# A decoder layer on one core: the gates' columns on ScalarE, a later place for the seventh mixed values, a new order in the first up tile, two more weight places

## The chip, the core and the metric

The kernel runs on one core of a Trainium2 chip. The metric is the device time of one execution in microseconds (us), the median of several runs. The engines are TensorE (PE in the profile: matmuls, and PEld: its weight loads), VectorE (DVE), ScalarE (ACT), GpSimd (POOL) and SyncE (SP), which issues nearly all of the DMAs.

## The reference

One decoder layer with 1024 rows of 1024 values, all in float32. Two groups of eight heads of 64 read one common input projection: sliding-window attention (window 128, two key heads, a sink per head) and forgetting attention, whose logits get the difference of running sums of log-sigmoid gates. Their outputs, joined to 1024 columns (the mixed values), go through `w_out` and are added to `x`. A feed-forward part with a squared ReLU follows.

```python
proj = jnp.einsum('bsd,de->bse', rmsnorm(x, attn_norm_g), w_in)
...
log_f = jax.nn.log_sigmoid(f_logit.astype(jnp.float32) + b_forget.astype(jnp.float32))
out_b = forgetting_attention(qb, kb, vb, log_f)
mixed = jnp.concatenate([out_a.reshape(b, s, A_Q_W), out_b.reshape(b, s, B_W)], axis=-1)
x = x + jnp.einsum('bse,ed->bsd', mixed, w_out)
hn = rmsnorm(x, mlp_norm_g)
hid = jnp.square(jax.nn.relu(jnp.einsum('bsd,df->bsf', hn, w_up)))
x = x + jnp.einsum('bsf,fd->bsd', hid, w_down)
```

## The kernel before

Every matrix product is made from two halves of each operand, a high one (the value rounded to the fp32r format) and a low one (the rest), in three matmuls: high by high, high by low, low by high. The function `split` makes the halves: a copy (ACT mostly) gives the high one, a subtraction (DVE or POOL) the low one. All matmuls of the products are recorded at line 73 and all splits of this function at lines 77 (ACT) and 80 (DVE, POOL), so that in the profile the tile names tell them apart.

The order of the instructions is not the order of the text. The program is traced, and a scheduler then lists each engine's instructions by priority and by the times that it expects; `high_priority` raises the priority of a block, and `issue_after(mark)` ties a block's instructions behind an earlier instruction of the same engine. On the chip every engine, and SP with its DMAs, follows its list in order.

**Input projection.** After the first 384 columns, `wa1_tile(t)` (line 458) projects row block t of 128 rows to 392 columns: 384 of queries and keys, and 8 that are the gates of the forgetting heads. `proj` uses two PSUM buffers in turn (pool `pd`), 24 matmuls each. ACT copies the 384 columns to `q3` (line 462). DVE reads the 8 columns, multiplies by the row's 1/rms (`rstd`), adds the bias `bfb`, and writes `z[:, :, t]` (line 463). The buffer is free when both have read it. `forget_gates` (line 470) turns `z` into running sums: a chain of DVE instructions on 64 columns, a transpose on PE (`ptf`, line 492), a scan, and a store to `c_d` (line 508).

**Attention** runs in units (scores, softmax, transposes, weighted sum), with the projections of the next heads, and later the first halves of the out projection, as fillers between them.

**Out projection.** For each of the eight column blocks dt, `out_first(dt)` does mixed blocks e = 0 to 3 beside the attention. `out_weights(dt, e0)` loads a piece of weights `wor` (two buffers), and splits it on ACT and POOL into a place w0 or w1, in turn. Places are slots of the pool `zw`, w0 to w6; a slot is given again when the last reader of its former tile is done. The variable i counts the pieces from 1; pieces 9 and 10 are those of dt = 0 and 4 with e = 4 to 7, whose products are spread by `beside(n, mark, e)` over the end of the attention, n being 0 or 1 for dt = 0 or 4. Six matmuls belong to each e. `drain` emits the waiting attention units, and `ended[-1]` is the last matmul of the newest of them. The seventh mixed values (e = 6) come through DRAM (`load_mix(6)`), the eighth (e = 7) straight from the last units. Pieces 11 to 16 follow for dt = 1, 5, 2, 6, 3, 7.

**The end of the out projection.** `out_finish(dt, ps)` adds the stored first half and writes h to DRAM. It then makes the inputs of the up projection, which uses Strassen's scheme (in Winograd's form) on 2 x 2 blocks: seven products whose right sides are sub-blocks of the scaled h (in `bh[1]`, `bh[2]`, `bh[3]`) and sums of them, t1 to t4, in `ts[:, 0]` to `ts[:, 3]`. Of each right side dt modulo 4 is a quarter. `ts[:, 0]` needs only dt below 4, the other sums need both halves. `sum_splits` splits a sum into `bh` and `bl`: sum 0 for product 5, 3 for 4, 1 for 6, 2 for 7. Before, all four are split when dt is 4 or more, and those for products 5 and 4 of the last quarter wait in `part["rest"]` until product 2 of the first up tile has been emitted. h of dt below 4 lies in w2, of dt 4 to 6 in w3.

**Up projection.** `up(j)` (16 tiles) makes four sums of weight blocks and then, in the order `UP = (1, 2, 3, 6, 7, 5, 4)`, splits the weights of each product into the next of the seven places (w5 first, then w6, w0, w1, w2, w3, w4), multiplies (12 matmuls, inputs in four quarters k) and adds the product into `u` and `b`.

**Down projection** follows, from about 784 us to the end.

Of the kernel before, what the change touches and what calls it, by code (L numbers as in the profile page):

```python
# [16 lines left out]
P = 128  # L17
# [38 lines left out]
def hybrid_layer(  # L56
# [89 lines left out]
    def slot(tag, name, shape, dt=F32, pool=None):  # L146
        pool = o[pool or ("zw" if tag[0] == "w" else "zl")]
        return pool.tile([P] + shape, dt, tag=tag, name=name, bufs=1)
# [309 lines left out]
    def wa1_tile(t):  # L458
        with paced():
            ps = proj(wa1, 392, t)  # L460
        with tc.high_priority(offset=HPA):
            nc.scalar.copy(q3[:, t, :], ps[:, :384])
            nc.vector.scalar_tensor_tensor(  # L463
                out=z[:, :, t], in0=ps[:, 384:392], scalar=rstd[:, t : t + 1], in1=bfb,
                op0=ALU.mult, op1=ALU.add,
            )
            if t % 2:
                qknorm(q3, 6, t - 1, t + 1)

    def forget_gates():  # L470
        zf = z.rearrange("p h t -> p (h t)")

        zt = ap2.tile([P, 4, NT * NH], F32, tag="sq", name="zt", bufs=1)
        ze, zs, zp = zt[:, 0], zt[:, 1], zt[:, 2]
        nc.vector.scalar_tensor_tensor(out=ze, in0=zf, scalar=-1.0, in1=zf, op0=ALU.mult, op1=ALU.min)
        nc.scalar.activation(ze, ze, AF.Exp)
        nc.vector.tensor_scalar(out=zs, in0=ze, scalar1=2.0, scalar2=None, op0=ALU.add)
        nc.vector.reciprocal(zs, zs)
        nc.vector.tensor_tensor(out=zs, in0=zs, in1=ze, op=ALU.mult)
        nc.vector.tensor_tensor(out=ze, in0=zs, in1=zs, op=ALU.mult)  # L480
        nc.vector.tensor_scalar_mul(zp, ze, 2.0 / 17.0)
        for n in (15, 13, 11, 9, 7, 5, 3):
            nc.vector.scalar_tensor_tensor(
                out=zp, in0=zp, scalar=2.0 / n, in1=ze, op0=ALU.add, op1=ALU.mult
            )
        nc.vector.scalar_tensor_tensor(out=zp, in0=zp, scalar=2.0, in1=zs, op0=ALU.add, op1=ALU.mult)
        nc.vector.scalar_tensor_tensor(
            out=zt[:, 3], in0=zf, scalar=0.0, in1=zp,
            op0=ALU.min, op1=ALU.subtract,
        )  # L490
        pt = pa.tile([P, 512], F32, tag="tr", name="ptf", bufs=3)
        nc.tensor.transpose(pt[: NH * NT, :P], zt[:, 3], ident)
        cum = ap2.tile([P, 256], F32, tag="mt", name="cum", bufs=2)[: NH * NT, :P]
        nc.vector.tensor_tensor_scan(
            out=cum, data0=ones1[: NH * NT].to_broadcast([NH * NT, P]),
            data1=pt[: NH * NT, :P], initial=0.0, op0=ALU.mult, op1=ALU.add,
        )
        off = pa.tile([P, 512], F32, tag="tr", name="off", bufs=3)
        mm(
            off[: NH * NT, 0:1], before.rearrange("p h t -> p (h t)"),  # L500
            cum[:, P - 1 : P], True, True,
        )
        offs = ap3.tile([NH * NT, 1], F32, name="offs")
        nc.vector.tensor_copy(offs, off[: NH * NT, 0:1])
        nc.vector.tensor_scalar(
            out=cum, in0=cum, scalar1=offs[:, 0:1], scalar2=None, op0=ALU.add
        )
        nc.sync.dma_start(c_d.rearrange("h (t q) -> (h t) q", q=P), cum)
# [357 lines left out]
    def out_weights(dt, e0):  # L866
        i = nout[0] = nout[0] + 1
        wr = o["zw"].tile([P, 4, P], F32, tag="wor", name="wor", bufs=2)
        nc.sync.dma_start(wr, w_o[dt][:, e0 : e0 + 4, :])
        w = slot(f"w{i % 2}", "wos", [2, 4, P], F32R)  # L870
        split(w[:, 0], w[:, 1], wr, nc.scalar, nc.gpsimd)
        return w[:, 0], w[:, 1]

# [51 lines left out]
    def beside(n, mark, *es):  # L925
        _, ps, w = ahead_of[n]
        with tc.issue_after(mark):
            out_products(ps, w, es)

    beside(0, marks[-1], 4, 5)  # L930
    beside(0, ended[-1], 6)
    beside(1, ended[-1], 4)
    drain(1)
    beside(1, ended[-1], 5)
    drain(0)
    beside(1, ended[-1], 6)
    for dt, ps, w in ahead_of:
        out_products(ps, w, [7])
# [25 lines left out]
    def out_finish(dt, ps):  # L964
        t, gain = dt % 4, gm[:, dt : dt + 1]
        h = slot(f"w{2 + dt // 4}", "h", [S]) if dt < 7 else rr
        with tc.issue_after(part["load"].ins) if dt == 7 else nullcontext():
            part["load"] = nc.sync.dma_start(h, part_d[dt])
        for c, cs in enumerate((left, right)):
            nc.vector.tensor_tensor(out=h[:, cs], in0=ps[c], in1=h[:, cs], op=ALU.add)  # L970
        nc.sync.dma_start(h_d[dt], h)
        if dt < 4:
            h_split(1, t, h[:, left], gain)
            ts = part["t"] = slot("m4", "ts", [4, 512])
            b12 = part["b12"] = slot("w4", "b12", [512])
            nc.scalar.activation(b12, h[:, right], AF.Copy, scale=gain)
            nc.vector.scalar_tensor_tensor(
                out=ts[:, 0], in0=h[:, left], scalar=gain, in1=b12, op0=ALU.mult, op1=ALU.subtract
            )
            return  # L980
        ts, b12 = part["t"], part["b12"]
        h_split(2, t, h[:, left], gain)
        h_split(3, t, h[:, right], gain)
        for i, q, other, op in (
            (1, right, ts[:, 0], ALU.add),
            (2, right, b12, ALU.subtract),
            (3, left, ts[:, 1], ALU.subtract),
        ):
            nc.vector.scalar_tensor_tensor(
                out=ts[:, i], in0=h[:, q], scalar=gain, in1=other, op0=ALU.mult, op1=op  # L990
            )
        part["rest"] = lambda: sum_splits(ts, t, ((0, 5), (3, 4)))
        sum_splits(ts, t, ((1, 6), (2, 7)))
        if t < 3:
            part.pop("rest")()
# [47 lines left out]
    def up(j):  # L1043
# [8 lines left out]
        minus(s[:, 3], a12, s[:, 1])  # L1052
        src = {1: a11, 2: a12, 3: s[:, 3], 4: a22, 5: s[:, 0], 6: s[:, 1], 7: s[:, 2]}
        m = {}
        for n in UP:
            w = w_slot("wu", [2, 4, P], F32R)
            split(w[:, 0], w[:, 1], src[n], nc.scalar, nc.vector if n in (2, 6, 5) else nc.gpsimd)
            m[n] = bank(f"pu{n}")
# [6 lines left out]
            if n == 1:  # L1065
                u = slot("m1", "u", [4, 512])
                b = slot("m2", "hb", [4, 512])
                nc.scalar.copy(u[:, 0], m[1])
            if n == 2:
                plus(b[:, 0], m[2], u[:, 0])  # L1070
            if n == 6:
                plus(u[:, 1], m[6], u[:, 0])
            if n == 7:
                plus(u[:, 2], m[7], u[:, 1])
            if n == 5:
                minus(u[:, 3], u[:, 1], m[5])
                minus(b[:, 2], u[:, 2], m[5])
                plus(b[:, 3], m[3], u[:, 3])
            if n == 4:
                plus(b[:, 1], m[4], u[:, 2])  # L1080
        return lambda: up_end(j, b)

    def up_end(j, b):
        nc.scalar.activation(b, b, AF.Relu)
# [273 lines left out]
```

## Time and profile before

| | |
|---|---|
| median of 3 runs | 1093.94 us (1093.51 to 1095.36) |
| profiled execution | 1094.93 us, its span 1093.2 us |
| granted clock of TensorE | 1.00 |
| DMA moved | 195.69 MB, 179 GB/s over the span |
| start of the first up product on PE | 476.59 us |
| start of the down products on PE | 783.96 us |

A row of the timeline has a start, a duration (both in us), the engine, the line, the operation, what it writes and reads, and a count where several were merged; in brackets stand the idle time before it and what ended it. A row of the waits has the total, the number of times and the longest.

### The profile page before, as it was taken

Reading aid. Unit: us, or ns where it says so; the run is one execution under the profiler, and the core shown is the slowest. Engines: PE = TensorE matmul, PEld = TensorE weight load, DVE = VectorE, ACT = ScalarE, POOL = GpSimd, SP = SyncE. Lnnn points to the kernel's source line nnn. Section 1 sums busy time; section 2 is a strip of 40 time slices with the busy share of each in tenths; the row PEclk is TensorE's granted clock in tenths of the full one; section 3 lists DMA queues with packets and bytes.
Section 4 is the critical chain, followed back from the end, with each engine's and each line's share of the span. In section 5 each row is a group of like instructions: output and inputs, shape, how many; then the busy total and the mean of one; then the engine's idle time right before and its main releaser. Section 6 shows DMA issues by size and latency. Waiting matters only on the chain.

```text
span 1093.2 us, 15691 instructions
## 1 busy us (share of the span) xinstructions
PE 1080.2 (99%) x5556; PEld 933.4 (85%) x5556; DVE 770.2 (70%) x1328; ACT 570.6 (52%) x1014; POOL 364.0 (33%) x352
## 2 busy tenths in 40 slices
PE   9999999999999999999999999999999999999998
PEld 8999999999998888888888888888888888888886
DVE  8377677766765676898686869665665877674395
ACT  5558588676765756554545453443633433333331
POOL 5572523435444544233223232332222222231100
PEclk9999999999999999999999999999999999999999
DMA  9401212324666465563554543344898876665423
GB/s 296 152 22 52 69 38 63 115 78 150 202 210 222 163 225 175 199 244 118 185 192 180 181 166 135 144 174 144 314 393 315 306 289 227 233 226 183 176 89 116
DMA packets 96223, 195.69 MB, mean 179 GB/s; under 512 B 7392, under 2 KB 19856, under 8 KB 96144
## 3 DMA queue, kind: packets, MB, share of 16 engines
q1 hardware_dynamic: 95856, 194.54, 51.4%
q8 instruction: 44, 0.72, 0.3%
q14 instruction: 35, 0.29, 0.1%
q10 hardware_dynamic: 288, 0.15, 0.0%
HBM read 141.61 MB, written 53.04 MB: 178 GB/s over the span
## 4 chain that ended last, share of the span: by engine, by line
PE 84%; DVE 6%; DMA 5%; issue 2%; ACT 2%; POOL 1%; SPq 0%; DVEq 0%; ACTq 0%
PE pu L73 28%; PE pd L73 27%; PE ps L73 12%; PE po L73 5%; PE spb L73 3%; PE pvb L73 3%; PE tpb L737 2%; PE sp L73 1%; PE pv L73 1%; DMA wr<-in_w_b_dram 1%; DMA xq<-in_x_dram 1%; PE tpa L566 1%; DVE x L217 1%; PE ptk L334 1%; DMA h_d<-h 1%
## 5 line engine op out<-in xcount | busy, mean ns | idle before, releaser
L73 PE MATMUL pd<-hx,wx 128*128 128x512 f32 (+1 forms) x1350 | 304.9, 388 | 0.0
L73 PEld LDWEIGHTS pd<-hx,wx 128*128 128x128 f32 x1350 | 252.7, 188 | 52.2
L73 PE MATMUL pu<-bh,wu 128*128 128x512 f32 x896 | 276.6, 390 | 0.5 <-ACT bh L959 0.5
L73 PE MATMUL ps<-w,x 128*128 128x384 f32 (+1 forms) x960 | 199.4, 345 | 1.5 <-DVE z L463 1.1
L73 PEld LDWEIGHTS pu<-bh,wu 128*128 128x128 f32 x896 | 168.1, 188 | 36.1 <-ACT bh L959 0.9
L73 PE MATMUL pu<-bl,wu 128*128 128x512 f32 x448 | 174.0, 389 | 0.0
L73 PEld LDWEIGHTS ps<-w,x 128*128 128x128 f32 x960 | 165.1, 189 | 5.0 <-DVE z L463 1.8
L77 ACT CAST hx<-hr 128x1024 fp32r<-128x1024 f32 x56 | 59.0, 1054 | 175.9 <-PE pd L73 169.9
L80 POOL TENSOR_TENSOR wx<-wda,wx 128x1024 fp32r<-128x1024 f32 x24 | 64.2, 2676 | 196.7 <-ACT wx L77 169.5
L80 DVE TENSOR_TENSOR hx<-hr,hx 128x1024 fp32r<-128x1024 f32 x56 | 72.6, 1305 | 72.6 <-ACT hx L77 72.6
L73 PEld LDWEIGHTS pu<-bl,wu 128*128 128x128 f32 x448 | 84.1, 188 | 17.6 <-issue 0.2
L73 PE MATMUL po<-mix,wos 128*128 128x512 f32 x384 | 95.0, 396 | 2.0 <-DMA mix<-mixs_d 1.1
L80 POOL TENSOR_TENSOR wu<-wus,wu 128x512 fp32r<-128x512 f32 x32 | 46.7, 1461 | 126.6 <-ACT wu L77 114.2
L73 PEld LDWEIGHTS po<-mix,wos 128*128 128x128 f32 x384 | 70.5, 188 | 16.7 <-ACT wos L77 1.5
L80 POOL TENSOR_TENSOR wu<-wur,wu 128x512 fp32r<-128x512 f32 x32 | 44.9, 1402 | 86.5 <-ACT wu L77 86.3
L77 ACT CAST wu<-wus 128x512 fp32r<-128x512 f32 x64 | 38.1, 617 | 62.3 <-PE pu L73 54.0
L1030 DVE TENSOR_TENSOR ht<-hb 128x512 f32<-128x512 f32 x32 | 21.8, 722 | 63.4 <-ACT hb L1085 63.4
L80 POOL TENSOR_TENSOR w<-wr,w 128x384 fp32r<-128x384 f32 (+1 forms) x47 | 51.3, 1100 | 41.3 <-ACT w L77 30.4
L406 DVE TENSOR_TENSOR ptl<-tpb,pth 128x512 fp32r<-128x512 f32 (+1 forms) x80 | 49.6, 631 | 21.9 <-ACT pth L405 18.7
L77 ACT CAST wx<-wda 128x1024 fp32r<-128x1024 f32 x56 | 58.5, 1049 | 7.1 <-DMA wda<-in_w_d_dram 7.1
L701 ACT ACTIVATE sb<-sb,nmb 128x128 f32<-128x128 f32 (+3 forms) x64 | 49.8, 778 | 22.5 <-DVE nmb L695 22.3
L405 ACT CAST pth<-tpb 128x512 fp32r<-128x512 f32 (+1 forms) x80 | 41.7, 543 | 16.9 <-PE tpb L737 11.0
(210 smaller groups left out, 1820.7 us busy)
## 6 DMA issues: line engine op xcount, KB each, us to landing
wda<-in_w_d_dram SPq DMA_DIRECT2D x34, 1024.0 KB, 8.8
hr<-hid_d SPq DMA_DIRECT2D x56, 512.0 KB, 5.9
wur<-in_w_u_dram SPq DMA_DIRECT2D x32, 512.0 KB, 4.3
hid_d<-ht SPq DMA_DIRECT2D x16, 1024.0 KB, 4.3
hid_d<-hb SPq DMA_DIRECT2D x16, 768.0 KB, 3.6
mix<-mixs_d SPq DMA_DIRECT2D x7, 1024.0 KB, 5.8
wr<-in_w_b_dram SPq DMA_DIRECT2D x32, 192.0 KB, 2.5
xq<-in_x_dram SPq DMA_DIRECT2D x8, 512.0 KB, 5.4
```

The costliest lines, as they stand in the source:

```text
L73: return nc.tensor.matmul(out, lhsT, rhs, start=start, stop=stop)
L77: hi_eng.copy(hi, src)
L80: lo_eng.tensor_tensor(out=lo, in0=src, in1=hi.bitcast(F32), op=ALU.subtract)
L217: last_x = nc.vector.scalar_tensor_tensor(out=lo, in0=xr[:, cs], scalar=ga, in1=hi.bitcast(F32), op0=ALU.mult, op1=ALU.subtract,)
L334: nc.tensor.transpose(pt[:w, j * P : (j + 1) * P], x[:, 4 * c + j, col : col + w], ident)
L405: nc.scalar.copy(hi[:, cols], pt[:, cols])
L406: nc.vector.tensor_tensor(out=lo[:, cols], in0=pt[:, cols], in1=hi[:, cols].bitcast(F32), op=ALU.subtract)
L566: nc.tensor.transpose(tp[:, hh * P : (hh + 1) * P], pts[hh // 2][:, hh % 2, c0 : c0 + P], ident)
L701: nc.scalar.activation(pr[:, :nk], pr[:, :nk], AF.Exp, scale=-1.0, bias=nm[:, c : c + 1], accum_out=dn_b[p % 2][:, h, i : i + 1] if p < 3 ...
L737: nc.tensor.transpose(tp[:, c0 : c0 + P], probs[qi][:, kb * P : (kb + 1) * P], ident)
L1030: eng.tensor_tensor(out=out, in0=a, in1=b, op=ALU.subtract)
```

## The change

Four edits. The 8 gate columns are read by ACT, scaled by `rstd`, and the bias is added later for all 64 columns at once by DVE. The six products of dt = 0 with e = 6 move behind the last drained unit. Pieces 11 and 12 of the out weights get the places w6 and w5. In the first up tile product 5 comes second; the sums of products keep their former order, each as soon as all before it are there (`todo`, `up_sums`), and sum 0 of each quarter (t1) is split when dt is below 4.

```diff
         with tc.high_priority(offset=HPA):
             nc.scalar.copy(q3[:, t, :], ps[:, :384])
-            nc.vector.scalar_tensor_tensor(
-                out=z[:, :, t], in0=ps[:, 384:392], scalar=rstd[:, t : t + 1], in1=bfb,
-                op0=ALU.mult, op1=ALU.add,
+            nc.scalar.activation(
+                z[:, :, t], ps[:, 384:392], AF.Copy, scale=rstd[:, t : t + 1]
             )
...
     def forget_gates():
+        nc.vector.tensor_tensor(
+            out=z, in0=z, in1=bfb.unsqueeze(2).to_broadcast([P, NH, NT]), op=ALU.add
+        )
...
-        w = slot(f"w{i % 2}", "wos", [2, 4, P], F32R)
+
+        w = slot(f"w{i % 2 + (5 if i in (11, 12) else 0)}", "wos", [2, 4, P], F32R)
...
     beside(0, marks[-1], 4, 5)
-    beside(0, ended[-1], 6)
     beside(1, ended[-1], 4)
     drain(1)
     beside(1, ended[-1], 5)
     drain(0)
+    beside(0, ended[-1], 6)
     beside(1, ended[-1], 6)
...
                 out=ts[:, 0], in0=h[:, left], scalar=gain, in1=b12, op0=ALU.mult, op1=ALU.subtract
             )
+            sum_splits(ts, t, ((0, 5),))
             return
...
-        part["rest"] = lambda: sum_splits(ts, t, ((0, 5), (3, 4)))
+        part["rest"] = lambda: sum_splits(ts, t, ((3, 4),))
...
-        for n in UP:
+        todo = list(UP)
+        for n in UP if j else (1, 5, 2, 3, 6, 7, 4):
             w = w_slot("wu", [2, 4, P], F32R)
...
             if n == 1:
                 u = slot("m1", "u", [4, 512])
                 b = slot("m2", "hb", [4, 512])
-                nc.scalar.copy(u[:, 0], m[1])
-            if n == 2:
-                plus(b[:, 0], m[2], u[:, 0])
...
+            while todo and todo[0] in m:
+                up_sums(todo.pop(0), m, u, b)
         return lambda: up_end(j, b)
+
+    def up_sums(n, m, u, b):
+        if n == 1:
+            nc.scalar.copy(u[:, 0], m[1])
+        if n == 2:
+            plus(b[:, 0], m[2], u[:, 0])
...
```

The rest of `up_sums` is the former list of sums, unchanged.

More of the change, by code (lines that the diff above doesn't have):

```diff
@@ L1067, in up @@
                 b = slot("m2", "hb", [4, 512])
-                nc.scalar.copy(u[:, 0], m[1])
-            if n == 2:
-                plus(b[:, 0], m[2], u[:, 0])
[L1071 to L1080, printed above, removed]
-        return lambda: up_end(j, b)
+            while todo and todo[0] in m:
+                up_sums(todo.pop(0), m, u, b)
+        return lambda: up_end(j, b)
+    def up_sums(n, m, u, b):
[3 more added lines that the diff above has]
+            plus(b[:, 0], m[2], u[:, 0])
+        if n == 6:
+            plus(u[:, 1], m[6], u[:, 0])
+        if n == 7:
+            plus(u[:, 2], m[7], u[:, 1])
+        if n == 5:
+            minus(u[:, 3], u[:, 1], m[5])
+            minus(b[:, 2], u[:, 2], m[5])
+            plus(b[:, 3], m[3], u[:, 3])
+        if n == 4:
+            plus(b[:, 1], m[4], u[:, 2])
     def up_end(j, b):
```

## The prediction

> **What bounds the kernel now.** The page comes first: the busy times of the engines.
>
> ```profile
> span 1093.2 us, 15691 instructions
> PE 1080.2 (99%) x5556; PEld 933.4 (85%) x5556; DVE 770.2 (70%) x1328; ACT 570.6 (52%) x1014; POOL 364.0 (33%) x352
> ```
>
> PE is the bound, and the change leaves its matmuls as many and as long as they were. So the change can win only where PE stands idle, 13.0 us in all. Next come PE's own waits.
>
> ```profile
> PE ps L73 <- DVE z L463: 1.1, 2, 0.8
> PE po L73 <- DMA mix<-mixs_d: 1.1, 1, 1.1
> PE po L73 <- ACT wos L77: 1.0, 2, 0.7
> PE pu L73 <- ACT bh L959: 0.5, 1, 0.5
> PE sp L73 <- DVE z L463: 0.5, 1, 0.5
> ```
>
> The columns are total, times and longest. Each of the four edits has its counterpart here: z is the gates' column, mix the mixed values, wos the weight places, bh the inputs of the first up tile. Then the windows say whether time won would last.
>
> ```profile
> 428.00:445.00 17.00, 15.22 (x84) 12.56 (x85) 9.91 (x19) 8.49 (x18) 2.26 (x7) 1.00 0.27 99
> ...
> 470.00:480.00 10.00, 9.49 (x43) 7.53 (x41) 10.00 (x17) 5.65 (x10) 0.00 (x0) 1.00 0.82 273
> ...
> 784.00:1084.00 300.00, 300.00 (x1325) 248.40 (x1324) 198.64 (x175) 113.12 (x113) 59.40 (x22) 1.00 0.67 240
> ```
>
> Columns: PE, PEld, DVE, ACT, POOL, clock, DMA share, GB/s. The clock is full. The last 300 us before the end are PE alone without a gap: what PE wins earlier ends at the end of the kernel. In 470 to 480 DVE is busy without a gap as well, so there an edit that gives DVE more to do early can cost.
>
> **Edit 1: the gates' columns go to ScalarE.** The timeline of PE shows the three waits, those of ACT and DVE what lies at the second and third.
>
> ```profile
> 47.77 2.94 PE L73 MATMUL ps<-w,x 128*128 128x392 f32 x15 [0.34 <-DVE z L463]
> ...
> 68.76 3.29 PE L73 MATMUL ps<-w,x 128*128 128x392 f32 x17 [0.80 <-DVE z L463]
> ...
> 78.95 0.36 PE L73 MATMUL sp<-k1a,q1a 128*128 128x256 f32 x1 [0.47 <-DVE z L463]
> ```
>
> ```profile
> 66.88 0.21 ACT L297 ACTIVATE sr<-ss 128x12 f32<-128x12 f32 x1
> 67.12 0.48 ACT L462 COPY q<-ps 128x384 f32<-128x384 f32 x1
> ```
>
> ```profile
> 68.48 0.23 DVE L463 SCALAR_TENSOR_TENSOR z<-ps,rstd,vt 128x8 f32<-128x8 f32 x1
> ...
> 78.72 0.09 DVE L545 DVE_READ_ACCUMULATOR2_ANT nm_a<- 128x1 f32 x1
> 78.72 0.23 DVE L463 SCALAR_TENSOR_TENSOR z<-ps,rstd,vt 128x8 f32<-128x8 f32 x1
> ```
>
> The projection has two PSUM buffers, and each is free only when both readers are done: the copy of 384 columns (ACT) and z (DVE). For the fifth row block ACT is through by 67.60, but z stands in DVE's queue until 68.48 and ends at 68.71; PE, out of work at 67.96, starts at 68.76. With z behind the copy on the same engine, the buffer is free by 67.12 + 0.48 + 0.21 = 67.81, before PE asks. The price of z on ACT is not in the trace; the nearest row, an ACT instruction of 12 columns, takes 0.21 against 0.23 on DVE. The bounds are 0.21 and the 0.48 of the whole copy; I take 0.21. Even at 0.48 the buffer is free at 68.08, and 0.12 of the wait stays. So 0.34 + 0.80 go. The third wait names z, yet the scores need a buffer that L545 frees; its last piece ends at 78.81 and PE starts at 78.95. Between nothing and 0.47, I take the difference of those two, 0.14. Sum of this edit: 1.28.
>
> The Trainium skill, "ScalarE: Activation LUTs", section "Rules for kernel authors", speaks against it: additions and multiplications belong on VectorE, which is up to about three times faster per element in bf16. By that rule alone z on ACT would cost three times its 0.23, and at 67.60 + 0.69 = 68.29 the second wait would keep 0.33. The rows do not agree (0.21 beside 0.23), because so short an instruction is not paid by the element; the rule would leave the edit at 0.95 instead of 1.28.
>
> The bias is now added to all 64 columns by one more DVE instruction at the head of the gates. Its price is that of the last instruction of the same shape:
>
> ```profile
> 120.13 0.23 DVE L487 SCALAR_TENSOR_TENSOR zt<-z,zt 128x64 f32<-128x64 f32 x1
> ...
> 122.42 0.27 PE L492 MATMUL ptf<-ident,zt 128*64 128x128 f32 x1
> ```
>
> The work that hides it is PE's projection: PE turns the gates 2.06 us after DVE has them. Without that cover it would cost 0.23.
>
> **Edit 2: the seventh mixed values last.** Timeline of PE, then of DVE, then the chain that ended last.
>
> ```profile
> 433.30 1.55 PE L73 MATMUL po<-mix,wos 128*128 128x512 f32 x6
> 435.91 1.66 PE L73 MATMUL po<-mix,wos 128*128 128x512 f32 x6 [1.06 <-DMA mix<-mixs_d]
> 437.40 0.28 PE L73 MATMUL pvb<-pth,vb 128*128 128x256 f32 x1
> ...
> 438.84 4.27 PE L73 MATMUL po<-mix,wos 128*128 128x512 f32 x18
> ```
>
> ```profile
> 433.95 0.56 DVE L406 TENSOR_TENSOR ptl<-tpb,pth 128x384 fp32r<-128x384 f32 x1 [0.77 <-ACT pth L405]
> ```
>
> ```profile
> 430.90 4.97 DMA mix<-mixs_d
> ```
>
> At 434.85 PE runs dry, since the next six products need the seventh mixed values, whose load lands at 435.87. Behind them stand twelve products of the last attention unit (437.40 to 438.84 by their starts, 1.44 us), whose operands are complete at 433.95 + 0.56 = 434.51. The change puts these twelve in front: they fill 434.85 to about 436.3, the load has landed, and the whole 1.06 goes. The margin is 436.3 - 435.87 = 0.4 us; a load later than that is waited for again. The mixed values of the last unit must now be ready after twelve more products (six before), so they have more cover than they had.
>
> **Edit 3: two more weight places.**
>
> ```profile
> 443.80 32.95 PE L73 MATMUL po<-mix,wos 128*128 128x512 f32 x144 [0.69 <-ACT wos L77]
> ```
>
> ```profile
> 443.15 1.12 ACT L77 CAST wos<-wor 128x512 fp32r<-128x512 f32 x2
> ```
>
> ```profile
> 422.18 0.33 SPq L869 DMA_DIRECT2D wor<-in_w_o_dram  x1
> ```
>
> ```profile
> DMA to landing us min/median/max: 2.9/3.7/7.9
> ```
>
> The last line is from the view of the tile wor. Weight pieces 11 and 12 were loaded by about 426 (422.18 + 3.7), but their places w1 and w0 held pieces 9 and 10 until PE's last product. In w6 and w5 nothing lies, and the two casts can run any time before 443. The 0.69 goes. POOL's half of the splitting moves with them:
>
> ```profile
> 443.83 3.08 POOL L80 TENSOR_TENSOR wos<-wor,wos 128x512 fp32r<-128x512 f32 x2 [10.07 <-ACT wos L77]
> ```
>
> ```profile
> 445.68 1.78 DVE L977 SCALAR_TENSOR_TENSOR ts<-h,vt,b 128x512 f32<-128x512 f32 x1
> ...
> 454.77 0.75 DVE L977 SCALAR_TENSOR_TENSOR ts<-h,vt,b 128x512 f32<-128x512 f32 x1
> ```
>
> The same DVE instruction takes 1.78 beside POOL and 0.75 without it, so the move gives a full DVE about 1.0 us back. I book none of it, as PE does not wait there. The Trainium skill, "GPSIMD Engine Reference", Specifications, has GpSimd share its SBUF interfaces with VectorE, in conflict with instructions of two SBUF inputs; the two rows agree. By that rule the earlier place does little harm, as the evictions of the attention tail (L406) read PSUM and only one SBUF input.
>
> **Edit 4: the first up tile in the order 1, 5, 2, 3, 6, 7, 4, with product 5's inputs split as soon as t1 is there.**
>
> ```profile
> 476.59 0.39 PE L73 MATMUL pu<-bh,wu 128*128 128x512 f32 x1
> ...
> 479.98 0.73 PE L73 MATMUL pu<-bh,wu 128*128 128x512 f32 x2 [0.51 <-ACT bh L959]
> ```
>
> ```profile
> 478.68 0.62 ACT L77 CAST wu<-wus 128x512 fp32r<-128x512 f32 x1 [1.80 <-DMA h_d<-h]
> 479.21 0.72 ACT L959 ACTIVATE bh<-h,vt 128x512 fp32r<-128x512 f32 x1
> ...
> 486.06 0.63 ACT L77 CAST wu<-wus 128x512 fp32r<-128x512 f32 x1 [1.25 <-DMA h_d<-h]
> ```
>
> PE waits for the fourth quarter of bh1, and that stands on ACT behind the cast of product 5's weights, which waits until h has left place w3. Now product 5 has w6, free long before, and nine of its products need only the first three quarters: 9 x 0.229 (32.95 / 144) = 2.06 us of cover for a wait of 0.51. It goes. Against it: PE comes 1.06 + 0.69 = 1.75 us earlier than before, while DVE, full, has its start moved by the 1.06 alone; the 0.69 are inside the 2.06 as well. DVE gets four low halves earlier, but three of them leave its list before the last h, so one (about 0.7 us) stands ahead; again covered.
>
> What is late next is place w2: product 7 used it, now product 6 does, one product earlier. It was free at 486.06. By the order of the text PE asks for it at 476.59 - 1.75 + 48 x 0.229 = 485.8, so the wait is 486.06 + 0.63 - 485.8 = 0.9 if h leaves no earlier, and nothing if it moves along with PE. Near the lower end, for h's sums come at least 1.06 earlier: I take 0.3.
>
> **Sum.** 1.28 + 1.06 + 0.69 + 0.51 = 3.54, less 0.3: 3.2 us. The profiled execution took 1094.93 us, 1.7 more than its span; it becomes 1091.7. It lies 1.0 above the median of the runs (1093.94), so the median becomes 1090.7.
>
> **Rivals.** About 0.2%, or 2.2 us, is what a measurement of this kernel can tell from no change.
>
> *New waits in the old places.* Product 6 pays its full 0.9 at w2, and the weight loads that now go earlier share the DMA engines with the load of the seventh mixed values. Two pieces of 256 KB (128 x 4 x 128 values of 4 bytes) at the 273 GB/s of the window of 470 to 480 take 1.9 us; if the load loses all of that, PE waits 1.9 - 0.4 = 1.5. The gain shrinks to 3.54 - 2.4 = 1.1: 1092.8. For it: ACT's 1.80 and 1.25 on h. Against it: in 428 to 445 the DMA engines are busy 0.27 of the time.
>
> *The time won at the gates is lost again.*
>
> ```profile
> 137.25 0.44 PE L73 MATMUL ps<-w,x 128*128 128x384 f32 x1 [0.31 <-ACT w L77]
> ```
>
> Here PE waits for weights whose load stands on SP behind the store of the gates' sums. If that chain kept its hour, this wait would grow by 1.28 and the gain would be 1.9: 1092.0. Against it: the chain goes through PE's own list (ptf at 122.42) and moves along.
>
> *Slower.* SP issues in order. The loads of pieces 13 and 14 wait until POOL has split 11 and 12, and these may now stand on SP ahead of the load of the seventh mixed values. That decides if the split of piece 11 stays late on ACT: at 441 the load would land at 441 + 5.0 = 446 instead of 435.87, PE would stand about 9.7 us from 436.3, and the kernel would take 6.2 us longer: 1100. From 5.8 us of delay on (3.54 + 2.2) it is slower by over 0.2%. Against it: these casts are free to run by 426, and ACT has room.
>
> *The change doesn't do what it says.* The order is worked out by a scheduler with times of its own; the trace shows the first tile's products already interleaved. If the two reorderings change nothing on PE (1.06 and 0.51 stay), the gain is 1.7: 1092.3. Against it: the six products are tied behind the last unit's mark, so they cannot stay.
>
> **How the numbers follow.** The forecast 0.64; new waits 0.11; lost at 137 0.09; no reordering 0.08; slower 0.08. Faster by over 0.2% is the forecast, within 0.2% are the three in the middle: 0.28. The range: down to 1089.2 (all of 3.87 with the third z wait whole, the 0.4 by which the fastest run lies under the median, and 0.5 for waits that the reshuffled schedule may drop), up to 1093.3 (new waits, with 0.5 for waits that it may add). It leaves out the slower case and some 0.1 at the ends.
>
> **What would show it.** Right: no PE wait on z, none on mix after 434, none on wos near 443, none on bh L959; the out products begin about 1.75 us earlier against the attention's end. Wrong: PE waits on DMA mix again, on ACT wu in the first up tile, or a larger wait on ACT w near 137; for the slower case a load of mix issued on SP behind two of wor.

## The result and the profile after

The change made the kernel slower. The median is 1099.86 us (1098.77 to 1100.64, 8 runs) against 1094.45 us of the kernel before in the same comparison (1093.42 to 1098.77, 8 runs): a ratio of 1.0045, interval 1.0034 to 1.0056. The forecast was 3.2 us faster; it came out 5.4 us slower. The profiled execution took 1100.15 us.

Two lines of the page of the kernel after, the span and the engines' busy times:

```profile
span 1098.4 us, 15693 instructions
...
PE 1083.5 (99%) x5556; PEld 938.1 (85%) x5556; DVE 776.2 (71%) x1321; ACT 573.7 (52%) x1022; POOL 369.6 (34%) x352
```

The span grew by 5.2 us. PE idles 14.9 us instead of 13.0 (the span less its busy time), and is busy 3.3 us longer with as many matmuls: more than half of the loss lies in matmuls that became slower. The waits of PE after (total, times, longest):

```profile
PE pu L73 <- ACT bh L962: 3.3, 1, 3.3
PE tpb L739 <- DVE ptl L406: 2.6, 3, 1.8
PE qps L73 <- DVE warm L191: 1.3, 1, 1.3
PE spb L73 <- DVE nmb L697: 0.8, 1, 0.8
PE pvb L73 <- DVE mtb L756: 0.7, 2, 0.5
```

Every wait that the four edits aimed at in the earlier part is gone: none on z, none on mix, none on wos. In their place stand two new ones: on `ptl`, the low half of the transposed probabilities near the end of the attention, and on `bh`, where 0.5 became 3.3. The windows around both (PE, PEld, DVE, ACT, POOL, clock, DMA share, GB/s):

```profile
415.00:430.00 15.00, 12.27 (x70) 10.19 (x69) 11.81 (x26) 10.42 (x23) 8.88 (x13) 0.89 0.46 158
480.00:490.00 10.00, 6.69 (x23) 5.19 (x22) 8.30 (x14) 5.71 (x10) 1.87 (x2) 0.83 0.72 281
```

PE loses 2.7 of 15 and 3.3 of 10 us, and the granted clock falls to 0.89 and 0.83. The timeline of PE shows what that does:

```profile
78.56 0.35 PE L73 MATMUL sp<-k1a,q1a 128*128 128x256 f32 x1 [0.46 <-DVE nm_a L547]
...
417.34 0.66 PE L739 MATMUL tpb<-ident,sb 128*128 128x128 f32 x4 [1.80 <-DVE ptl L406]
...
419.23 0.58 PE L73 MATMUL pvb<-pth,vb 128*128 128x256 f32 x1 [0.55 <-DVE mtb L756]
419.61 0.41 PE L73 MATMUL pvb<-ptl,vb 128*128 128x256 f32 x1
...
477.37 0.39 PE L73 MATMUL pu<-bh,wu 128*128 128x512 f32 x1
...
483.57 1.05 PE L73 MATMUL pu<-bh,wu 128*128 128x512 f32 x2 [3.31 <-ACT bh L962]
484.41 0.63 PE L73 MATMUL pu<-bl,wu 128*128 128x512 f32 x1
...
487.54 0.39 PE L73 MATMUL pu<-bl,wu 128*128 128x512 f32 x1
```

After the 3.31 us a matmul takes 0.63 and not 0.39, and one starts every 0.43 us instead of every 0.23; from 487.54 they are fast again. Eight matmuls at 0.2 us too much are 1.6 us on top of the wait. The same is seen from 419.61: 0.41 where such a matmul takes 0.28. What held the two producers up stands in ACT's timeline:

```profile
413.10 0.62 ACT L77 CAST wos<-wor 128x512 fp32r<-128x512 f32 x1 [3.77 <-DMA wor<-in_w_o_dram]
...
415.98 0.59 ACT L405 CAST pth<-tpb 128x512 fp32r<-128x512 f32 x1
...
417.71 0.62 ACT L77 CAST wos<-wor 128x512 fp32r<-128x512 f32 x1 [1.15 <-DMA wor<-in_w_o_dram]
...
482.27 0.62 ACT L77 CAST wu<-wus 128x512 fp32r<-128x512 f32 x1 [2.77 <-DMA h_d<-h]
482.80 0.72 ACT L962 ACTIVATE bh<-h,vt 128x512 fp32r<-128x512 f32 x1
```

In both places ACT stands still in front of a cast whose input, or whose place, is not there yet, and the eviction or the input that PE needs stands behind that cast. At 413.10 it is the cast of piece 11, for 3.77 us: edit 3 let it go ahead of piece 10's, and its load, the eleventh of `wor`, was issued only at 408.95. At 417.71 it is that of piece 12; at 482.27 it is the cast of product 7's weights into w3, which waits until h of column block 6 has left that place. SP's timeline has the load and, further on, that write of h:

```profile
408.95 0.38 SPq L871 DMA_DIRECT2D wor<-in_w_o_dram  x1
...
474.96 0.32 SPq L974 DMA_DIRECT2D h_d<-h  x1
475.37 2.89 SPq L1016 DMA_DIRECT2D wur<-in_w_u_dram  x4
```

The write was issued at 472.21 before and at 474.96 now, 2.4 us instead of 4.4 ahead of the first up product, with four weight loads right behind it in both kernels. The cast came 6.5 us behind it before (478.68) and 7.3 now.

### The profile page after: what moved, and what is told of

Read it like the earlier page. It is cut to its first block, busy times and chain, and to the rows that moved or that the text cites. A ratio compares the mean times of both kernels' runs of the same rounds, so it can differ in the third digit from the quotient of the medians.

```text
span 1098.4 us, 15693 instructions
## 1 busy us (share of the span) xinstructions
PE 1083.5 (99%) x5556; PEld 938.1 (85%) x5556; DVE 776.2 (71%) x1321; ACT 573.7 (52%) x1022; POOL 369.6 (34%) x352
## 4 chain that ended last, share of the span: by engine, by line
PE 89%; DMA 5%; DVE 3%; issue 1%; ACT 1%; SPq 1%; POOL 0%; DVEq 0%; ACTq 0%; POOLq 0%
PE pu L73 28%; PE pd L73 27%; PE ps L73 14%; PE po L73 4%; PE qps L73 3%; PE pvb L73 3%; PE spb L73 3%; PE tpb L739 2%; PE sp L73 1%; PE pv L73 1%; PE tpa L568 1%; DMA h_d<-h 1%; PE ptk L334 1%; DMA wur<-in_w_u_dram 1%; DMA wor<-in_w_o_dram 1%
## 5 line engine op out<-in xcount | busy, mean ns | idle before, releaser
L80 POOL TENSOR_TENSOR wu<-wur,wu 128x512 fp32r<-128x512 f32 x32 | 49.7, 1555 | 105.0 <-ACT wu L77 105.0
L697 DVE CUSTOM_DVE_ANT_0 sb<-spb,cb 128x512 f32<-128x512 f32 (+2 forms) x64 | 37.2, 584 | 22.5 <-PE spb L73 17.4
```

Of the source, the lines that this page charges most:

```text
L80: lo_eng.tensor_tensor(out=lo, in0=src, in1=hi.bitcast(F32), op=ALU.subtract)
L697: nc.vector.tensor_tensor_reduce(out=pr[:, c * 512 : c * 512 + n], in0=sp[:, :n], in1=cb[:, c * 512 : c * 512 + n], scale=1.0, scalar=3e38 ...
```

## The experiments

Each was compared with the kernel before on its own chip, in five rounds; three chips were used, so the ratios compare better than the microseconds. Three repairs are made with `issue_after`: it only sets the order in one engine's list, behind a named instruction. T: ScalarE's casts of pieces 11 and 12 behind its copy in the last attention unit. W: the cast of product 7's weights (w3) in the first up tile behind `bh2` of the last column block. S: the weight sums of the first up tile on VectorE behind the adds of h of block 2. The fourth, L, moves the low half of product 4's weights in the first tile from POOL to VectorE.

| kernel | contents | median us | ratio to before, interval |
|---|---|---|---|
| gates_only | edit 1 | 1092.30 | 0.9972, 0.9961 to 0.9983 |
| mixed_last_only | edit 2 | 1094.10 | 0.9993, 0.9979 to 1.0007 |
| places_only | edit 3 | 1099.01 | 1.0032, 1.0018 to 1.0045 |
| up_order_only | edit 4 | 1098.24 | 1.0022, 1.0010 to 1.0033 |
| gates_and_mixed | edits 1, 2 | 1093.38 | 0.9983, 0.9973 to 0.9993 |
| places_tied | edit 3, T | 1097.30 | 1.0024, 1.0014 to 1.0035 |
| places_sums_later | edit 3, T, S and product 2's split | 1096.23 | 1.0012, 0.9999 to 1.0025 |
| up_order_low4_vector | edit 4, L | 1094.03 | 0.9997, 0.9982 to 1.0012 |
| gates_w3_later | edit 1, product 5's cast moved | 1093.74 | 0.9986, 0.9977 to 0.9996 |
| after_tail_casts_tied | all, T | 1094.65 | 1.0005, 0.9995 to 1.0015 |
| w3_later | all, W | 1096.65 | 1.0020, 1.0011 to 1.0029 |
| all_repaired | all, T, W, L | 1093.07 | 0.9982, 0.9972 to 0.9991 |
| all_repaired_sums | all, T, W, L, S | 1091.65 | 0.9965, 0.9953 to 0.9977 |
| all_repaired_sums_2 | the same, another chip | 1091.70 | 0.9974, 0.9963 to 0.9984 |
| mended_without_order | edits 1, 2, 3, T, S and product 2's split | 1093.39 | 0.9991, 0.9982 to 1.0001 |
| mended_without_places | edits 1, 2, 4, W, L | 1091.99 | 0.9973, 0.9962 to 0.9983 |

### One edit at a time

**gates_only**

```diff
-            nc.vector.scalar_tensor_tensor(out=z[:, :, t], ...
+            nc.scalar.activation(z[:, :, t], ps[:, 384:392], AF.Copy, scale=rstd[:, t : t + 1])
```

> Edit 1 alone: the gates' columns are read by ScalarE, nothing else is changed. Theory A (the loss comes from casts that stand in ScalarE's list ahead of other work and wait for a transfer: the weight casts of pieces 10 to 12 in the attention tail, and the cast of product 7's weights ahead of bh1): edit 1 has no part in it, the waits on z go, 1.2 us faster than before, PE waits between 405 and 440 no larger than before. Rival B (any edit near the front reshuffles the attention stage, and that is what costs): 1.5 to 2.5 us slower, with new PE waits in the attention tail.

Measured: 0.9972, more gained than either theory had. The gain was had although a wait grew; the waits of PE:

```profile
PE pu L73 <- ACT bh L961: 2.1, 1, 2.1
...
PE po L73 <- ACT wos L77: 0.7, 1, 0.7
```

No wait on z and none on mix is left. Edit 1 does what the prediction said, and it reshuffles the attention. The mix wait need not have gone by that: it is missing in up_order_only too, whose lists are those of the kernel before until past 460 us. The old 0.5 on bh has become 2.1, probably as PE comes earlier.

**mixed_last_only**

```diff
-    beside(0, ended[-1], 6)
     beside(1, ended[-1], 4)
...
+    beside(0, ended[-1], 6)
     beside(1, ended[-1], 6)
```

> Edit 2 alone: the six products with the seventh mixed values behind the last attention unit. Both theories: the wait of 1.06 us on the load of mix goes, 1.0 us faster; theory B would allow a loss only if other waits in the tail change.

Measured: 0.9993, which cannot be told from no change, nor from the forecast 1.06 us (0.1%). PE has the order that was meant, and the wait on mix is gone from the profile. But this wait comes and goes by itself: with the lists of the kernel before it is 1.06 there, 0.84 in places_tied and missing in up_order_only, so the profile doesn't show that the edit removed it.

**places_only**

```diff
-        w = slot(f"w{i % 2}", "wos", [2, 4, P], F32R)
+        w = slot(f"w{i % 2 + (5 if i in (11, 12) else 0)}", "wos", [2, 4, P], F32R)
```

> Edit 3 alone: places w6 and w5 for weight pieces 11 and 12. Theory A: the casts of pieces 11 and 12 move on ScalarE into the attention tail ahead of evictions and wait there for their load; PE waits on DVE ptl of 1.5 us or more between 410 and 425, followed by a time of slow matmuls; 1.5 to 3 us slower in spite of the 0.7 won at wos. Rival B: 0.7 us faster.

Measured: 1.0032. ACT's timeline has the casts ahead of the softmax and the evictions, waiting for their loads:

```profile
419.19 0.62 ACT L77 CAST wos<-wor 128x512 fp32r<-128x512 f32 x1 [1.33 <-DMA wor<-in_w_o_dram]
...
424.75 0.62 ACT L77 CAST wos<-wor 128x512 fp32r<-128x512 f32 x1 [2.10 <-DMA wor<-in_w_o_dram]
```

PE pays for it in four waits of 0.5 to 0.9 us at 428 to 433, on `dnb` and `ptl`, later than expected; and it has two waits of 1.0 us in the first up tile, which no theory had. The profiled execution, 1101.12 us, is the slowest of the seven.

**up_order_only**

```diff
-        for n in UP:
+        for n in UP if j else (1, 5, 2, 3, 6, 7, 4):
```

(with the sums and splits of the change's last hunks)

> Edit 4 alone: first up tile in the order 1, 5, 2, 3, 6, 7, 4. Theory A: the cast of product 7's weights stands ahead of bh1 on ScalarE and waits until h has been written; the PE wait on bh1 is as long as before (0.5) or longer, up to 3 us if the write of h is late, with slow matmuls behind it; between 0 and 3 us slower. Rival B: the cover of nine products of number 5 removes the wait, 0.5 us faster.

Measured: 1.0022. The wait on bh did not go, and a larger one came, neither theory's. The timelines of PE and of POOL:

```profile
479.04 0.73 PE L73 MATMUL pu<-bh,wu 128*128 128x512 f32 x2 [0.77 <-ACT bh L959]
...
495.71 0.73 PE L73 MATMUL pu<-bh,wu 128*128 128x512 f32 x2 [2.31 <-POOL wu L80]
```

```profile
486.65 9.00 POOL L80 TENSOR_TENSOR wu<-wur,wu 128x512 fp32r<-128x512 f32 x2 [6.76 <-ACT wu L77]
```

PE waits for the low weights of product 4. They are the second of these two subtractions on POOL, which take 9.00 us together and 1.3 each when VectorE leaves POOL alone. The first belongs to another product, and most of the time is its own: in up_order_low4_vector below, where product 4's has left POOL, it still takes 6.99. So here too an instruction that PE doesn't need yet stands in front.

### Taking the suspects away

**places_tied**

```diff
-        split(w[:, 0], w[:, 1], wr, nc.scalar, nc.gpsimd)
+        with tc.issue_after(copies[-1]) if i in (11, 12) else nullcontext():
+            split(w[:, 0], w[:, 1], wr, nc.scalar, nc.gpsimd)
```

> Edit 3 alone, as in places_only, but ScalarE's casts of pieces 11 and 12 are tied behind ScalarE's copy in the last attention unit (the places w6 and w5 and all else stay). Theory A (in places_only the casts stand in ScalarE's list ahead of the attention's evictions and wait there for their loads, and this makes TensorE wait): the waits of 0.5 to 0.9 us on ptl and dnb at 428 to 433 go, no wait on wos near 443 either, and the loss of 0.32% is gone: a ratio of 0.999 to 1.000, 1094 to 1095.5 us. Theory B (the places themselves, the earlier work of POOL or the loads of pieces 13 and 14 cost): it stays near 1.003, with the same waits; or a new wait on wor 13 and 14, whose loads now start about 20 us later, near 445 to 450.

Measured: 1.0024, a miss. The lists up to the end of the attention are those of the kernel before, and no wait on `ptl` or `dnb` over 0.6 is left; but the waits in the first up tile stay, and with them most of the loss. VectorE's timeline ahead of it:

```profile
466.06 1.31 DVE L80 TENSOR_TENSOR wu<-wur,wu 128x512 fp32r<-128x512 f32 x1 [0.73 <-ACT wu L77]
467.30 1.77 DVE L1035 TENSOR_TENSOR wus<-wur 128x512 f32<-128x512 f32 x1
469.00 0.68 DVE L1032 TENSOR_TENSOR wus<-wur 128x512 f32<-128x512 f32 x1
469.60 1.28 DVE L972 TENSOR_TENSOR h<-po,h 128x512 f32<-128x512 f32 x2
```

Three instructions of the first up tile now stand ahead of both adds of h of block 2; before, one of them stood between the adds and two behind. The first waits 0.73 for its cast, two are stretched to about 1.3 and 1.8 beside POOL. (This profile too is of the slowest of the seven executions, 1100.20 us.) All that VectorE has to do for h comes later, while PE comes earlier.

**places_sums_later**

```diff
+        with tc.issue_after(part["h2"]) if j == 0 else nullcontext():
             plus(s[:, 0], a21, a22)
...
+            with tc.issue_after(part["h2"]) if j == 0 and n == 2 else nullcontext():
                 split(w[:, 0], w[:, 1], src[n], ...
```

> Edit 3 with the tied casts of places_tied, and in addition the four weight sums of the first up tile and the split of its product 2 tied, on VectorE, behind the adds of h of column block 2 (on ScalarE nothing changes). In places_tied these come ahead of the adds: VectorE waits 0.7 us for the cast of product 2's weights, two of the three instructions are stretched to 1.3 and 1.8 us beside POOL, h of blocks 2 and 6 comes 1.2 to 1.5 us later, and TensorE waits 1.2 on bh and 1.1 on bl in the first up tile. Theory D (these three instructions in VectorE's list are edit 3's loss): the wait on bh goes to 0.5 or less, bl under 0.5, and the ratio falls from 1.0024 to 0.999 to 1.0005. Theory B (the later places of POOL's and ScalarE's work cost by themselves): the waits stay over 1 us each and the ratio at 1.002 or more.

Measured: 1.0012 (0.9999 to 1.0025), half way. PE's timeline in the first up tile:

```profile
481.89 0.73 PE L73 MATMUL pu<-bh,wu 128*128 128x512 f32 x2 [0.43 <-ACT bh L961]
...
492.38 0.73 PE L73 MATMUL pu<-bh,wu 128*128 128x512 f32 x2 [1.13 <-POOL wu L80]
```

The waits on bh and bl fell as theory D had it, but POOL is next: a wait of 1.13. So these three instructions are a part of the loss, and behind them there is another late engine.

**up_order_low4_vector**

```diff
-            ... nc.vector if n in (2, 6, 5) else nc.gpsimd)
+            ... nc.vector if n in (2, 6, 5) or n == 4 and j == 0 else nc.gpsimd)
```

> Edit 4 alone as in up_order_only, but the low half of product 4's weights in the first up tile is made by VectorE (0.68 us) and not by POOL; the lists are otherwise the same there. Theory P (edit 4's loss is POOL's subtraction, stretched from 1.3 to about 4.5 us beside a full VectorE): the wait of 2.3 us on POOL wu goes and with it the stretch of half clock behind it (14 matmuls of 0.43 instead of 0.23, some 2.5 us): ratio from 1.0022 to 0.9985 to 1.0. Theory Q (another instruction is as late: VectorE's own list): a wait of 1 us or more at the same product, ratio over 1.001.

Measured: 0.9997, theory P. The wait of 2.3 is gone, and with it the slow stretch (nine matmuls in up_order_only, not the 14 of the expectation); PE's list is that of up_order_only, and POOL's timeline shows that the stretch is real, on the instruction that stood in front of product 4's and that PE does not wait for:

```profile
486.58 6.99 POOL L80 TENSOR_TENSOR wu<-wur,wu 128x512 fp32r<-128x512 f32 x1 [7.11 <-ACT wu L77]
```

**w3_later**

```diff
+            with tc.issue_after(part[2]) if j == 0 and n == 7 else nullcontext():
                 split(w[:, 0], w[:, 1], src[n], ...
```

> The kernel after, with one cast moved: that of product 7's weights into w3 in the first up tile is tied behind ScalarE's bh2 of the last column block, so it stands no longer ahead of the last quarter of bh1. Theory A (this cast, waiting for the write of h out of w3, holds bh1 back): the wait of 3.3 us on bh goes to under 0.6, with it the stretch of matmuls of 0.63 us behind it (8 by 0.2 = 1.6 us). Then the wait of 2.3 us on the low weights of product 4 (POOL) as in up_order_only comes out, with its own slow stretch. Between 4.4 us (no new wait) and 0.5 us faster than the kernel after: ratio to the kernel before 1.000 to 1.004. Theory B (bh1 is late since h of dt 3 itself or VectorE's bl1 is late): a wait of 1 us or more on bh or bl stays at the same place.

Measured: 1.0020 against 1.0045 of the kernel after, theory A, with waits as PE's timeline shows:

```profile
478.30 0.73 PE L73 MATMUL pu<-bh,wu 128*128 128x512 f32 x2 [0.70 <-ACT bh L961]
...
494.59 0.73 PE L73 MATMUL pu<-bh,wu 128*128 128x512 f32 x2 [0.65 <-POOL wu L80]
```

The 3.31 became 0.70 (under 0.6 was expected), with no slow matmuls behind it; the wait on POOL came out, smaller than expected.

**gates_w3_later** (edit 1, and the same tie in the former order)

```diff
+            with tc.issue_after(part[2]) if j == 0 and n == 5 else nullcontext():
                 split(w[:, 0], w[:, 1], src[n], ...
```

> Edit 1 alone, with the cast of product 5's weights (place w3, former order) tied on ScalarE behind bh2 of the last column block. In gates_only TensorE waits 2.1 us on bh, since this cast stands ahead of bh1 and waits for the write of h. Theory A (the cast holds bh1 back in the former order as well): the wait on bh falls under 0.7, ratio from 0.9972 to 0.995 to 0.9965, 1089.5 to 1091.5 us. Rival: bh1 or bl1 is late by itself, since VectorE is full, or product 5's low weights then come late: a wait of over 1 us at bh, bl or wu, ratio 0.997 or more.

Measured: 0.9986, a miss, and the rival's case. The wait on bh went, but product 5's low inputs came late instead, in PE's timeline:

```profile
490.09 0.50 PE L73 MATMUL pu<-bl,wu 128*128 128x512 f32 x1 [1.65 <-DVE bl L80]
```

In the former order the wait only changes places, as VectorE is full.

**gates_and_mixed** (the two diffs above)

> Edits 1 and 2 alone. If the edits add up (theory A), the ratio is that of the two alone: 0.9972 x 0.9993 = 0.9965, 1091.6 us against 1095.4, with no wait on z and none on mix; since gates_only had lost its mix wait already, it may add nothing: 0.997. Theory C (each edit reshuffles the lists, and what comes out is chance): a ratio that lies outside 0.995 to 0.998, with waits that neither of the two had.

Measured: 0.9983, whose interval from 0.9973 up leaves out the product 0.9965 of the two. By its number that is theory C's case; by its waits it is not, for beside one of 0.32 on z none over 0.3 us is there that neither of the two had. Nothing is shown of a gain that edit 2 adds to edit 1.

**all_repaired** (T, W, L on the kernel after)

> All four edits, with three repairs: the casts of pieces 11 and 12 behind ScalarE's copy in the last attention unit, the cast of product 7's weights behind bh2 of the last column block, and the low half of product 4's weights in the first tile by VectorE and not POOL. Theory A (the loss is three instructions that stand at the wrong place in the list of an engine): no TensorE wait on ptl over 0.6, bh or wu; the gain foretold for the four edits comes at last, about 3.2 to 5 us under the kernel before: ratio 0.9955 to 0.997, 1090 to 1092 us. Theory C (what comes out of a reshuffle is chance): waits at other places eat it, ratio 0.998 or more.

Measured: 0.9982, by its number just inside theory C's range. The 3.31, the waits on POOL and those of the tail are gone; 0.83 on bh and 0.35 on bl are left, at the places where w3_later had them.

**all_repaired_sums** (and S)

> The kernel of all_repaired, with the four weight sums of the first up tile tied behind the adds of h of column block 2 on VectorE. Theory D: h of block 6 comes 1 to 1.5 us earlier against TensorE, the waits of 0.8 on bh and 0.35 on bl go, ratio from 0.9982 to 0.997. Rival (VectorE is full from 445 to 500, so what is moved behind one add is missing at the next): the waits only change places, ratio 0.998 or more.

Measured: 0.9965, theory D. In the waits of PE nothing over 0.2 us is left in the first up tile:

```profile
PE pu L73 <- DVE bl L964: 0.2, 1, 0.2
PE pu L73 <- ACT wu L77: 0.2, 1, 0.2
```

### How the loss and the gain divide

**after_tail_casts_tied** (T alone on the kernel after)

> The kernel after with one repair: the casts of pieces 11 and 12 behind ScalarE's copy in the last attention unit; the first up tile stays as it is. Theory A (casts that stand in ScalarE's list cost at the tail): the waits of 1.8 and 0.55 us on ptl and mtb and the slow transposes behind them go, the wait of 3.3 on bh stays, and the ratio falls from 1.0045 to 1.002 to 1.003. Rival (the tail costs nothing in the median, all of the loss is in the first up tile): 1.004 or more.

Measured: 1.0005 against 1.0045, more than expected. The two windows that answer to each other, the kernel after and then this one:

```profile
400.00:445.00 45.00, 41.67 (x241) 35.01 (x238) 29.14 (x68) 25.33 (x56) 15.69 (x27) 0.96 0.45 154
```

```profile
400.00:445.00 45.00, 44.01 (x258) 37.05 (x257) 31.72 (x72) 28.67 (x60) 18.87 (x25) 1.00 0.53 178
```

In the same 45 us PE is busy 2.3 us more, at full clock. The wait on bh is untouched, as PE's timeline has it:

```profile
478.31 0.90 PE L73 MATMUL pu<-bh,wu 128*128 128x512 f32 x2 [3.28 <-ACT bh L963]
```

**mended_without_order** (edit 4 undone in the mended kernel, product 5's cast in its old place, product 2's split tied as in places_sums_later)

```diff
-        for n in UP if j else (1, 5, 2, 3, 6, 7, 4):
+        for n in UP:
```

> Edits 1, 2 and 3 with the casts of pieces 11 and 12 tied and the sums and product 2's split of the first up tile behind h of block 2; edit 4 is left out (former order of the up products). If edit 4 is what gives edit 3's 0.7 us their cover: slower than all_repaired_sums_2 by 0.1% or more, with TensorE waits of 1 us or more in the first up tile. If the order is worth nothing: equal within 0.05%.

**mended_without_places** (edit 3 undone in the mended kernel, and with it T and S)

```diff
-        w = slot(f"w{i % 2 + (5 if i in (11, 12) else 0)}", "wos", [2, 4, P], F32R)
+        w = slot(f"w{i % 2}", "wos", [2, 4, P], F32R)
```

> Edits 1, 2 and 4 with product 7's cast behind bh2 and product 4's low half on VectorE; edit 3 is left out (places w0 and w1 for pieces 11 and 12). If the places bring their foretold 0.69 us: a wait of 0.6 to 0.7 on wos near 440 comes back and it is slower than all_repaired_sums_2 by about 0.06%, which the interval can hardly tell; if the places are worth nothing or less: equal or faster, 0.996 to 0.9965 against the kernel before.

**all_repaired_sums_2**

> The kernel of all_repaired_sums once more, beside the two that leave one edit out: 0.9965 within 0.001.

Measured, on one chip: 0.9991 without edit 4, 0.9973 without edit 3, 0.9974 with all. The order of the products with its repairs is worth about 0.17%, though the intervals still overlap a little; without it PE waits twice in the first up tile, 0.65 on bh and 0.64 on bl. The two places are worth nothing that these runs show (the 0.69 us would be 0.06%): without them PE waits 0.3 on wos, with them 0.4. The mended kernel, at 1091.7 in both comparisons, is the fastest of the four-edit kernels; whether gates_only (1092.3) differs from it, these runs cannot tell.

## Why the prediction was wrong

**The landmarks.** From the timelines of PE, in us:

| kernel | first up product | first down product | between | span |
|---|---|---|---|---|
| before | 476.59 | 783.80 | 307.2 | 1093.2 |
| after | 477.37 | 788.99 | 311.6 | 1098.4 |
| after_tail_casts_tied | 472.15 | 783.75 | 311.6 | 1093.2 |
| w3_later | 474.72 | 784.35 | 309.6 | 1093.8 |
| all_repaired_sums | 472.61 | 780.06 | 307.5 | 1089.5 |

(The table of the kernel before, ahead of the change, has 783.96 for its first down product; PE's timeline has 783.80.) By the forecast the first up product comes 1.28 + 1.06 + 0.69 = 3.0 us earlier than before. It came 0.8 later, 3.8 behind the forecast. T alone, which moves two casts in the tail of the attention, brings it to 472.15, somewhat beyond the forecast. The first up tile was to win 0.2 and lost 4.4: 3.31 instead of 0.51 of waiting (2.8), and 1.6 of slow matmuls. What lies behind the first up tile is unchanged, as the prediction said: from the first down product to the end it is 309.4 us in all five. One profile scatters: after and w3_later have the same lists up to the first up product and differ by 2.65 us there (the clock has a part in that, see the last section), so the ratios above decide, and they say the same: T is worth 0.40%, W 0.25%.

**Edit 1, right as a mechanism, and more in size.** Two rows of the windows, the kernel before and gates_and_mixed:

```profile
0.00:140.00 140.00, 136.33 (x810) 129.96 (x811) 95.82 (x257) 85.24 (x217) 71.42 (x85) 1.00 0.38 119
```

```profile
0.00:140.00 140.00, 137.47 (x820) 131.50 (x821) 96.19 (x252) 88.22 (x229) 70.72 (x86) 1.00 0.37 119
```

PE is busy 1.1 us more (1.7 in gates_only), against 1.28 foretold. The time gained is more: 0.28% is 3.1 us, and by the interval of gates_only at least 1.9. What the rest comes from is not shown; in gates_and_mixed and gates_w3_later, which have the edit too, 0.17 and 0.14% were gained. The instruction on ACT takes 0.28 where 0.21 was taken. Two details failed: the third wait of 0.47 was never due to z. The row at 78.56 shows it at 0.46 with the gates on ACT, on `nm_a`, so the 0.14 were not there to win. And gates_and_mixed still waits 0.32 once.

**Edit 2, not shown.** The wait on mix is gone wherever the edit was made, but also in gates_only and up_order_only, which do not have it. The step that failed is the 1.06 as a fixed price: it was read off one profile, and with the same lists the wait is 0 to 1.06 us. The edit alone gave 0.07%, which is not told from nothing.

**Edit 3, wrong.** The step that failed is "the two casts can run any time before 443", with "ACT has room". They can; but each engine follows a list made ahead of time, and a cast that is free earlier is put earlier. It then stands in the list and waits for its load (3.77 us for piece 11's), and what is behind it waits too, piece 10's cast among it. The prediction asked whether ACT had time, and not what would stand behind the casts. It named such a wait in one rival, for SP's queue and with the sign turned round, the casts staying late; the harm came from their going early. What was to show that rival is there, the load of mix is issued on SP at 432.75 behind two of wor at 419.71 and 421.41, but PE does not wait for mix. That its 1100 us are close to the measured 1099.86 is chance. A second cost lay in the first up tile: the 0.69 were "inside the 2.06", and the 2.06 were not there.

**Edit 4, wrong.** Two steps failed. "Nine of its products need only the first three quarters: 9 x 0.229 = 2.06 us of cover": they need no more, but PE's list is fixed, and it has three of them ahead of the fourth quarter of bh1: twelve matmuls from 477.37, nine of product 1 and three of product 5, and then PE stands. Before, twelve ran from 476.59 to the wait as well, so the new order gave no cover. And "that stands on ACT behind the cast of product 5's weights, which waits until h has left place w3. Now product 5 has w6": w3 has then another tenant, product 7, whose cast stands at the same point of ACT's list with the same wait. W shows that this cast was it. Place w2, priced at 0.3, cost nothing that a row shows; product 4's low weights, which stood on POOL behind a subtraction stretched beside a full VectorE and were not priced, cost 2.3 and a slow stretch in up_order_only.

**What was not in the sum at all** are the slow matmuls behind a wait. All terms were priced as idle time only.

**The alone and the together.** The four edits alone make -0.28, -0.07, +0.32 and +0.22, in sum +0.19%; together +0.45%. A likely reason, not tested by itself, is that PE comes earlier by edit 1 and the same late casts then hold it up for longer. Mended, the four give 0.9965 and 0.9974, which is 0.26 to 0.35%, or 2.8 to 3.8 us: about the 3.2 us that were forecast. Term by term this agreement is partly luck: edit 1 gave more than its 1.28, edits 2 and 3 nothing that can be shown, and edit 4 with its repairs 0.17% (1.9 us) where 0.51 less 0.3 were priced. Nor is the mended kernel told from gates_only. No run has the repairs on the kernel before, so what they would give without the edits is open. It is shown that moving single instructions in the lists gives the loss back; why the scheduler lists them so was only argued (it takes the loads to land earlier than they do).

## What to carry over

An instruction that becomes free to run earlier is not free of cost: it may be listed earlier, and then it stands in its engine's queue, in front of work that PE is waiting for, until its own load or place is there. So for each instruction that a change lets go earlier, ask what it waits for, what would stand behind it, and tie it behind a late instruction of its engine if it need not be early. And if a wait stands at a place (here w3), ask who has that place after the change; giving the old tenant another one does not move the wait.

## What the hardware showed beyond that

**A wait of PE can cost more than its length.** After 3.31 us of idling matmuls took 0.63 instead of 0.39 for 3.4 us, after 2.31 in up_order_only as well, with a granted clock of 0.50 in the window of 498 to 500; 1.80 with 0.55 behind it was enough at 417. A wait of 2.15 in gates_only had no slow matmul behind it, nor had those of 1.0 to 1.2 us in places_only and places_tied. So no single length decides in these runs.

What decides can be read off the traces. Between the first microseconds and the last products each slow stretch in them lasts 3.41 us at a clock of 0.50, and the two of the kernel after begin at 418.94 and 483.79, 64.85 us apart, 19 times 3.413: the clock changes in steps of a fixed grid. The windows of the steps right ahead of the five slow stretches, and of two places where the clock held:

| kernel | step, us | PE busy in it, of 3.41 us | clock of the next step |
|---|---|---|---|
| after | 480.38 to 483.79 | 0.22 | 0.50 |
| after_tail_casts_tied | 475.29 to 478.70 | 0.39 | 0.50 |
| up_order_only | 493.53 to 496.94 | 1.23 | 0.50 |
| after | 415.53 to 418.94 | 1.35 | 0.50 |
| places_only | 335.71 to 339.12 | 1.69 | 0.50 |
| gates_w3_later | 487.55 to 490.96 | 1.76 | 1.00 |
| gates_only | 473.02 to 476.44, then to 479.85 | 2.28, then 2.40 | 1.00 |

In all 18 traces a step at full clock with PE idle for 1.72 us or more is followed by a slow one, and none with 1.65 or less is. The wait of 2.15 in gates_only lies across the end of a step, so each of the two has only a part of it. A wait of about 2 us thus costs some 1.6 us more, or nothing, by where it falls on the grid. That is also a part of the scatter: after has 2.06 us of idling in one step of the tail, w3_later has 1.03 and 0.90 in two and no slow stretch; and the one of places_only at 339 lies ahead of anything that its edit moves. This is read off one profile of each kernel, and no run was made to test it.

The Trainium skill, "TensorE: Matmul & The Clock Gate", section "Why this matters for your kernels", warns of idle gaps beyond about 3 us between bursts; here the clock fell after 2.31 and after 1.80 too, and the measurement decides.

**POOL beside a full VectorE.** A subtraction of 128 x 512 on POOL takes 1.3 us, and 6.99 in up_order_low4_vector, while VectorE ran without a gap, nearly always an instruction with two SBUF inputs. The Trainium skill, "Trainium Architecture — The Big Picture", section "What this means for kernel authors", says that the two engines share a pair of ports by an exclusive lock and not by dividing the bandwidth; the row agrees (halves would make 2.6 of the 1.3), and the prediction, which drew on the sharing, had looked only at what POOL does to VectorE.
